# A decoder layer on one core: out projection with the model's columns on partitions, the second norm's square put onto the MLP's sums later, x1 turned by VectorE blocks and HBM

## The chip, the cores and the metric

The kernel runs on one core of one Trainium2 chip. The metric is the device time of one execution in microseconds (us); the time before is the median of three runs. Engines are named as in the profile: PE is TensorE, DVE is VectorE, ACT is ScalarE, POOL is GpSimd, and SP is the queue that issues nearly all DMAs.

## The reference

One layer of a causal decoder, for 1024 tokens (T) of 1024 columns (D), in float32. With `DEPTH = 1` only layer 0 runs: gated linear attention (GLA), then an MLP, then a last norm.

```python
x = x + gla_mixer(rms_norm(x, norm_mix), ...)      # ends in (o * silu(r)) @ w_out
x = x + sqrelu_mlp(rms_norm(x, norm_ffn), w1, w2)  # square(relu(h @ w1)) @ w2
return rms_norm(x, final_norm)
```

`rms_norm(x, g)` is x times rstd = (mean of x squared + 1e-6) to the power -1/2, one number per token, times g, one number per column. The x after the mixer is called x1 below. Two things follow from the formula and are used by the change: a positive factor per token passes through relu, and comes out of the square as its square. So the MLP of rstd * (x1 * g) is rstd squared times the MLP of x1 * g.

## The kernel before

The last part of the kernel, from line 908, is one out projection (1024 x 1024 x 1024) and an MLP whose 4096 hidden columns are worked in four chunks (NC = 4) of 1024; each chunk is an up projection (1024 x 1024 x 1024) and a down projection of the same size, whose sums are added up over the chunks. These nine matrix products are the entries 0 to 8 of the list `plan`: the out projection is 0, the up projections are 1, 3, 5, 7, the down projections 2, 4, 6, 8.

Each product is cut in halves along all three sizes (blocks "11", "12", "21", "22") and made by Strassen-Winograd's scheme: seven block products instead of eight. A block product is a **step** of 48 matmuls of 128x128 by 128x512: four lanes (128 rows of the result), four slices of the inner size, and three matmuls for each of these, because every float32 operand is split into a high and a low float32r part (`split`, lines 79 to 82: ScalarE copies the high part, VectorE subtracts for the low part). A step is named by its product number n; `PLAIN` (line 140) runs them in the order 0, 5, 1, 2, 3, 4, 6, `USUAL` in the order of their numbers. "Step 5" in the texts below is the position in this order, counted from 0. Before a step its two operands are made: the block sums of the scheme (`Side.sums`, line 180, each a 128x1024 instruction on VectorE or GpSimd) and the split into tiles called `big`. There are eight `big` tiles, four to a step, so the operands of a step can be made while the step before it runs, when the step before that has let go of its tiles.

A product's left side is either the weights or the activations, given by the flag s_form and the order in the tuple of `plan`: it sets which formulas of `form` (line 147) each side uses. After a step, its **sink** takes each lane's result out of PSUM: onto x1 (`onto_x1`, line 936), into the hidden tiles (`hidden_into`, line 980) or into the last norm (`final`, line 1028).

The order on TensorE is written by hand: it is the order of the program text, and `hooks` puts further work at a place (product, step, lane, slice) or behind a step's preparation ("then"). On the other engines and on SP the compiler's scheduler orders the instructions by readiness and by place in the text; they run in that order.

Around the change the work is this:

- The out projection has the tokens on partitions: the gated output og (four `hq` tiles, called qk there) is the left side, w_out the right side. Its sums are added onto x1, which is x loaded into eight `vx` tiles, one for each 128 tokens (`load_x1`, line 932).
- When a token tile is complete, `normed` (line 960) makes its square sum on ScalarE (L963), rstd (`rstd_of`, lines 103 to 114), and x1 times rstd on VectorE (L965). Then `transposed` (line 968) turns it by TensorE: 64 transposes of 128x128 (L975), whose results ScalarE scales with g_ffn into four `hq` tiles xraw (L977). The `hooks` of lines 1077 to 1079 place these transposes in the last steps of the out projection and the first steps of the first up projection.
- The first up projection makes its right-hand operands from xraw. `keep_w` (line 1005) stores all 14 split tiles (1 MB each) in HBM as xw, and the later three up projections only load them again, two for each step (`Stored`, lines 1009 to 1021, L1019).
- Every down projection adds its sums onto x1 by `onto_x1` (L940), the last one inside `final`, which squares, norms and stores the rows.

Buffers that matter: `hq` 4, `vx` 8, `raw` 2, `g4` 6, `big` 8 (line 56). In PSUM there are eight banks, `gl` 5 and `mm` 3.

Of the kernel before, what the change touches and what calls it, by code (L numbers as in the profile page):

```python
# [16 lines left out]
P = 128  # L17
T = 1024
# [30 lines left out]
def hybrid_trunk(ctx: ExitStack, tc: tile.TileContext, x, xT, w_head, w_r, w_gk, w_up,  # L49
# [69 lines left out]
    def run(general):  # L119
# [8 lines left out]
        def half(hf):  # L128
            return slice(hf * 512, hf * 512 + 512)
# [778 lines left out]
        def from_out(a, b, kh, dst):  # L908

            load = nc.sync.dma_start(dst.rearrange("p (h n) -> p h n", h=2),  # L910
                              w_out[4 * b + 2 * a:4 * b + 2 * a + 2, :, half(kh)].rearrange("h p n -> p h n"))
            order_after(tc, load, box["xt", 7, R_LAST[0]], wait=False)

        def from_up(c):
# [12 lines left out]
            return bring  # L927


        x1 = {}  # L930

        def load_x1(t):
            x1[t] = new("vx")
            order_after(tc, nc.sync.dma_start(x1[t], x[t * P:(t + 1) * P, :]), box["xt", 7, R_LAST[1]], wait=False)

        def onto_x1(n, lane, p_):
            e, dh = int(PART[n][0]) - 1, int(PART[n][1]) - 1
            xd = x1[4 * e + lane][:, half(dh)]
            with tc.high_priority():
                return dve.tensor_tensor(xd, p_, xd, op=ALU.add)  # L940

        def og_block(a, b):
            return lambda kp, n: qk[kp // 2, b - 1].rearrange("p (h t) -> p h t", h=2)[:, :, half(a - 1)]

        so = Side(True, {f"{a}{b}": og_block(a, b) for a in (1, 2) for b in (1, 2)}, dve, pair_temp, late=True)
        wo = weight_side(False, from_out, dve, "vx")
        wo.load("11")
        wo.load("21")
        ops = [[so.split(0), wo.split(0)]]
        for t in range(4):  # L950
            load_x1(t)
        wo.load("12")
        wo.load("22")
        for t in range(4, 8):
            load_x1(t)


        xn, xraw = {}, {}

        def normed(t):  # L960
            xt = new("g4")
            with tc.high_priority():
                act.activation(xt, x1[t], AF.Square, accum_out=ss2[:, t:t + 1])  # L963
                rstd_of(rstd2[:, t:t + 1], ss2[:, t:t + 1], 1, D)
                dve.tensor_scalar(xt, x1[t], rstd2[:, t:t + 1], None, op0=ALU.mult)  # L965
            xn[t] = xt

        def transposed(hf, kts):
            for kt in kts:
                b = f"{kt // 4 + 1}{hf + 1}"  # L970
                if b not in xraw:
                    xraw[b] = in_tile(new("hq"))
                p_ = new("mm")
                for c in range(4):
                    pe.transpose(p_[:, c * P:(c + 1) * P], xn[4 * hf + c][:, kt * P:(kt + 1) * P], ident)  # L975
                with tc.high_priority():
                    act.activation(xraw[b](kt % 4, 1)[:, 0, :], p_, AF.Copy, scale=g_ffn[:, kt:kt + 1])  # L977


        def hidden_into(hd):  # L980
# [28 lines left out]
        class Stored:  # L1009
# [5 lines left out]
            def split(self, n):  # L1015
                out = []
                for kh in range(2):
                    w = new("big", F32R)
                    nc.sync.dma_start(w.bitcast(F32), xw[n][kh])  # L1019
                    out.append(kl(w))  # L1020
                return out


        gfin = []
# [3 lines left out]
        def final(n, lane, p_):  # L1028

            e, dh = int(PART[n][0]) - 1, int(PART[n][1]) - 1  # L1030
            t = 4 * e + lane
            xt, rs = x1[t], rstd3[:, t:t + 1]
            onto_x1(n, lane, p_)
            if n in (3, 4):
                y, sq = row[t] = new(ROW[t])[:, 0:D], new("st")
                cs = half(dh)
# [28 lines left out]
        def norm_after(last, e):  # L1065
            def then(n, lane, p_):
                onto_x1(n, lane, p_)
                if n == last:
                    normed(4 * e + lane)
            return then  # L1070

        def load_gfin():
            gfin.append(new("g4"))
            nc.sync.dma_start(gfin[0], g_fin)


        hooks = {(0, 5, 3, 1): (0, (0, 1)), (0, 5, 3, 3): (0, (2, 3)), (0, 6, 0, 3): (0, (4, 5)), (0, 6, 1, 3): (0, (6, 7)),
                 (1, 0, 2, 3): (1, (0, 1)), (1, 0, 3, 1): (1, (2, 3)), (1, 0, 3, 3): (1, (4, 5)), (1, 1, 0, 1): (1, (6, 7))}
        hooks = {k: (g(transposed, *w),) for k, w in hooks.items()}
        hooks[0, 0, 3, 3] = (g(outputs_T, TT - 1, ("mm", "mm")),)  # L1080
        hooks[2 * NC - 2, 0] = (load_gfin,)
        chunks_of(plan, ops, hooks, {(0, 4): norm_after(3, 0), (0, 6): norm_after(6, 1)}, last_by_lane=True)

    flag = sb.tile([P, 1], I32, name="flag")
    with tc.manual_schedule(engines={mybir.EngineType.PE}):
# [67 lines left out]
```

## Time and profile before

| what | value |
|---|---|
| median of three runs | 1005.69 us (1005.55 to 1005.74) |
| the profiled execution | 1004.96 us, its span 1003.7 us |
| TensorE busy | 991.0 us, 99% |
| VectorE, ScalarE, GpSimd busy | 737.1, 554.6, 226.0 us |
| DMA | 176.87 MB in 98956 packets, mean 176 GB/s |
| share of the chain of waits on TensorE | 81%; 1% of it the transposes of L975 |

The profile shows one execution. The span is the time between its first and its last recorded instruction; the execution's own time is a little longer. "Busy" counts the time in which an engine has an instruction running. The chain of waits follows the work that ended last back to what released it each time: only what stands in the chain sets the end. A row of groups gives the source line, the engine, the operation, output and inputs, the shape, the count, the busy time, the mean of one in ns, and the idle time before it with what ended it. "PEclk" is the clock granted to TensorE, in tenths of full speed; it is at full speed nearly throughout.

### The profile page before, as it was taken

How to read it: one execution, taken by the hardware profiler on the slowest of the kernel's cores; microseconds unless marked ns; L12 is line 12 of the kernel's file. 1: busy time of each engine (PE TensorE's matmuls, PEld its weight loads, DVE VectorE, ACT ScalarE, POOL GpSimd, SP SyncE). 2: the span in 40 equal slices, each digit the busy share in tenths (PEclk: the TensorE clock that was granted, in tenths of full speed). 3: DMA queues.
4: the chain of work that ended last, by engine and by line, in shares of the span. 5: the costliest groups of instructions: out<-in, count | busy, mean ns of one | idle time of the engine just before them, and what ended most of it. 6: DMA issues, size and time to landing. Idle time of an engine off the chain costs nothing.

```text
span 1003.7 us, 12278 instructions
## 1 busy us (share of the span) xinstructions
PE 991.0 (99%) x4572; PEld 827.3 (82%) x4572; DVE 737.1 (73%) x899; ACT 554.6 (55%) x842; POOL 226.0 (23%) x142
## 2 busy tenths in 40 slices
PE   9999999999999999999999999999999999999995
PEld 8888878889988888888888888888888888888884
DVE  6995786778899998889873349874349964339965
ACT  7775554787793577666432546332447342456455
POOL 0000110113430000042233141234141224241270
PEclk9999999999999999999999999999999999999998
DMA  9899785576382224761215851214951224960004
GB/s 279 312 333 361 285 295 194 202 245 209 122 302 62 79 92 187 293 251 43 85 46 189 353 209 43 78 49 180 349 225 43 61 65 168 338 236 14 1 1 171
DMA packets 98956, 176.87 MB, mean 176 GB/s; under 512 B 5576, under 2 KB 67144, under 8 KB 87368
## 3 DMA queue, kind: packets, MB, share of 16 engines
q1 hardware_dynamic: 98328, 175.59, 49.0%
q8 instruction: 38, 0.62, 0.3%
q10 hardware_dynamic: 560, 0.40, 0.1%
q14 instruction: 30, 0.25, 0.1%
HBM read 138.23 MB, written 37.75 MB: 175 GB/s over the span
## 4 chain that ended last, share of the span: by engine, by line
PE 81%; ACT 2%; DVE 2%; issue 1%; ACTq 0%; DVEq 0%
PE gl L70 54%; PE mm L70 26%; PE mm L975 1%; PE mm L636 0%; ACT g L696 0%; DVE vx L940 0%; PE mm L715 0%; DVE big L82 0%; ACT wb L81 0%; DVE big L783 0%; ACT g L1045 0%; PE gl L715 0%; DVE g L705 0%; DVE g L675 0%; ACT hq L717 0%
## 5 line engine op out<-in xcount | busy, mean ns | idle before, releaser
L70 PE MATMUL gl<-big,big 128*128 128x512 f32 x2712 | 631.4, 390 | 0.3 <-DVE big L82 0.3
L70 PEld LDWEIGHTS gl<-big,big 128*128 128x128 f32 x2712 | 508.1, 188 | 105.8 <-DVE big L82 0.9
L70 PE MATMUL mm<-big,big 128*128 128x512 f32 x1224 | 288.2, 389 | 0.0
L70 PEld LDWEIGHTS mm<-big,big 128*128 128x128 f32 x1224 | 229.7, 188 | 47.7
L82 DVE TENSOR_TENSOR big<-wa,big 128x1024 fp32r<-128x1024 f32 (+1 forms) x120 | 162.1, 1376 | 103.8 <-ACT big L81 103.7
L81 ACT ACTIVATE big<-wa 128x1024 fp32r<-128x1024 f32 (+1 forms) x120 | 120.6, 1039 | 133.1 <-PE gl L70 63.4
L184 POOL TENSOR_TENSOR wa<-wa,wa 128x1024 f32<-128x1024 f32 x28 | 75.2, 2691 | 160.5 <-DVE big L82 159.6
L184 POOL TENSOR_TENSOR wa<-wa,wb 128x1024 f32<-128x1024 f32 x14 | 42.9, 3065 | 279.2 <-DVE big L82 279.2
L82 DVE TENSOR_TENSOR big<-wb,big 128x1024 fp32r<-128x1024 f32 x48 | 63.4, 1338 | 50.1 <-ACT big L81 50.1
L82 DVE TENSOR_TENSOR big<-hq,big 128x1024 fp32r<-128x1024 f32 x48 | 61.3, 1283 | 42.8 <-ACT big L81 42.8
L81 ACT ACTIVATE big<-wb 128x1024 fp32r<-128x1024 f32 x48 | 49.1, 1053 | 61.7 <-PE mm L70 31.0
L81 ACT ACTIVATE big<-hq 128x1024 fp32r<-128x1024 f32 x48 | 48.7, 1054 | 58.2 <-PE gl L70 32.5
L81 ACT ACTIVATE big<-raw 128x1024 fp32r<-128x1024 f32 x42 | 43.7, 1058 | 52.4 <-DVE raw L184 25.4
L82 DVE TENSOR_TENSOR big<-raw,big 128x1024 fp32r<-128x1024 f32 x42 | 66.8, 1607 | 2.3 <-ACT big L81 2.2
L940 DVE TENSOR_TENSOR vx<-gl,vx 128x512 f32<-128x512 f32 x95 | 63.2, 682 | 4.5 <-PE gl L70 4.3
L184 POOL TENSOR_TENSOR wa<-wb,wa 128x1024 f32<-128x1024 f32 x14 | 41.1, 2946 | 44.7 <-DVE big L82 44.7
L556 POOL COPY top<-g 128x4 f32<-128x4 f32 x8 | 10.1, 1264 | 180.6 <-DVE g L548 180.6
L998 ACT ACTIVATE hq<-hq 128x1024 f32<-128x1024 f32 x24 | 25.4, 1058 | 29.6 <-DVE hq L991 29.6
L678 POOL TENSOR_SCALAR g<-g,est 128x256 f32<-128x256 f32 x28 | 29.1, 1057 | 52.0 <-DVE g L675 33.0
L70 PE MATMUL gl<-wb,wa 128*128 128x256 f32 x180 | 32.1, 310 | 0.0
L940 DVE TENSOR_TENSOR vx<-mm,vx 128x512 f32<-128x512 f32 x45 | 30.1, 681 | 2.0 <-PE mm L70 1.9
L989 ACT ACTIVATE hq<-gl 128x512 f32<-128x512 f32 x36 | 21.3, 592 | 14.6 <-PE gl L70 14.6
(191 smaller groups left out, 834.6 us busy)
## 6 DMA issues: line engine op xcount, KB each, us to landing
big<-xw SPq DMA_DIRECT2D x42, 1024.0 KB, 6.8
big<-xv SPq DMA_DIRECT2D x20, 1024.0 KB, 6.1
xv<-big SPq DMA_DIRECT2D x14, 1024.0 KB, 7.5
xw<-big SPq DMA_DIRECT2D x14, 1024.0 KB, 5.8
wb<-in_w_ff SPq DMA_DIRECT2D x32, 256.0 KB, 3.3
wa<-in_w_ff SPq DMA_DIRECT2D x32, 256.0 KB, 3.4
wa<-in_w_ff SPq DMA_DIRECT2D x16, 512.0 KB, 4.5
wb<-in_w_ff SPq DMA_DIRECT2D x16, 512.0 KB, 4.3
```

Source lines behind the costliest of these rows:

```text
L70: pe.matmul(o, w, m, start=start, stop=stop, skip_group_check=partial)
L81: last["split"] = act.activation(hi, src, AF.Copy)
L82: last["low"] = dve.tensor_tensor(lo, src, f32(hi), op=ALU.subtract)
L184: op = self.eng.tensor_tensor(*(self.ap(b, kp, 2) for b in (o, x_, y_)), op=op)
L556: pool.tensor_copy(top[:, 8 * h + 4 * hf:8 * h + 4 * hf + 4].unsqueeze(2), a[:, :, P - 1:P])
L678: pool.tensor_scalar(S[:, vs], Z[:, vs], g, None, op0=ALU.mult)
L940: return dve.tensor_tensor(xd, p_, xd, op=ALU.add)
L975: pe.transpose(p_[:, c * P:(c + 1) * P], xn[4 * hf + c][:, kt * P:(kt + 1) * P], ident)
L989: act.activation(d, p_, AF.Copy)
L998: act.activation(d2, d2, AF.Relu)
```

## The change

The out projection changes its sides: w_out is now the left side (model columns on partitions) and og the right side, so that its result is x1 turned, x1T. It is added onto x turned, which the host lays out anyway (`load_x1T`, from xT). The 64 transposes, `normed` and `transposed` go away. `times_g` multiplies each finished half tile of x1T by g_ffn (per partition now) straight into xraw. No rstd is applied there: the MLP works on x1 * g.

The MLP's sums go into eight new tiles y (`onto_y`), opened in the first chunk by the sinks' first touch and not lying on x1 any more. x1 is wanted again with tokens on partitions. For this each finished x1T tile is stored to HBM (xh). In the second up projection it is loaded again (`turn_load`), each 32x32 block of it is transposed by VectorE (`turn_blocks`), and four DMAs for each tile (`turn_store`) put the blocks in their places of xm, rows of 32 floats at a time. In the fourth up projection `x1_load` brings xm back by token tiles, and `x1_onto` makes the square sum and rstd, squares rstd, and sets y to y * rstd^2 + x1. The last down projection's sums are multiplied by rstd^2 as they are added (in `final`).

The diff without the removed functions (`load_x1`, `onto_x1`, `normed`, `transposed`, `norm_after` and the old hooks):

```diff
-                              w_out[4 * b + 2 * a:4 * b + 2 * a + 2, :, half(kh)].rearrange("h p n -> p h n"))
+                              w_out[4 * a + 2 * b:4 * a + 2 * b + 2, :, half(kh)].rearrange("h p n -> p h n"))
...
+        def load_x1T(kt):
+            x1T[kt] = new("vx" if kt < 6 else "g4")
+            order_after(tc, nc.sync.dma_start(x1T[kt], xT[kt * P:(kt + 1) * P, :]), box["xt", 7, R_LAST[1]], wait=False)
+        def times_g(name, lane):
+            if name not in xraw:
+                xraw[name] = in_tile(new("hq"))
+            e, hf = int(name[0]) - 1, int(name[1]) - 1
+            kt = 4 * e + lane
+            act.activation(xraw[name](lane, 1)[:, 0, :], x1T[kt][:, half(hf)], AF.Copy, scale=g_ffn[:, kt:kt + 1])
+        def onto_x1T(n, lane, p_):
+            kt, hf = 4 * (int(PART[n][0]) - 1) + lane, int(PART[n][1]) - 1
+            xd = x1T[kt][:, half(hf)]
             with tc.high_priority():
-                return dve.tensor_tensor(xd, p_, xd, op=ALU.add)
+                dve.tensor_tensor(xd, p_, xd, op=ALU.add)
+                if n in (3, 4, 6):
+                    times_g(PART[n], lane)
+            if n in (3, 6):
+                nc.sync.dma_start(xh[kt], x1T[kt])
...
-        so = Side(True, {f"{a}{b}": og_block(a, b) for a in (1, 2) for b in (1, 2)}, dve, pair_temp, late=True)
-        wo = weight_side(False, from_out, dve, "vx")
+        so = Side(False, {f"{a}{b}": og_block(a, b) for a in (1, 2) for b in (1, 2)}, dve, pair_temp, late=True)
+        wo = weight_side(True, from_out, dve, "vx")
...
+        def turn_load(kt):
+            turn[kt] = new("g4")
+            order_after(tc, nc.sync.dma_start(turn[kt], xh[kt]), last["xw"], wait=False)
+        def turn_blocks(kt):
+            u = new("g4")
+            dve.transpose(u, turn[kt])
+            turn[kt] = u
+        def turn_store(kt):
+            u = turn.pop(kt)
+            for q_ in range(4):
+                dst = xm[:, kt * P + 32 * q_:kt * P + 32 * q_ + 32].rearrange("(b i) j -> i b j", i=32)
+                store = nc.sync.dma_start(dst, u[32 * q_:32 * q_ + 32, :].rearrange("p (b j) -> p b j", j=32))
+                order_after(tc, store, last["xw"], wait=False)
...
-                    nc.sync.dma_start(w.bitcast(F32), xw[n][kh])
+                    last["xw"] = nc.sync.dma_start(w.bitcast(F32), xw[n][kh])
...
+        def onto_y(c):
+            def add(n, lane, p_):
+                t, dh = 4 * (int(PART[n][0]) - 1) + lane, int(PART[n][1]) - 1
+                if t not in y_:
+                    y_[t] = new("vx")
+                yd = y_[t][:, half(dh)]
+                with tc.high_priority():
+                    if c == 0 and n in (0, 1, 2, 6):
+                        act.activation(yd, p_, AF.Copy)
+                    else:
+                        dve.tensor_tensor(yd, p_, yd, op=ALU.add)
+            return add
+        def x1_load(t):
+            x1m[t] = new("g4")
+            order_after(tc, nc.sync.dma_start(x1m[t], xm[t * P:(t + 1) * P, :]), last["xw"], wait=False)
+        def x1_onto(t):
+            sq, one_ = new("raw"), slice(t, t + 1)
+            act.activation(sq, x1m[t], AF.Square, accum_out=ss2[:, one_])
+            rstd_of(rstd2[:, one_], ss2[:, one_], 1, D)
+            dve.tensor_tensor(ss2[:, one_], rstd2[:, one_], rstd2[:, one_], op=ALU.mult)
+            dve.scalar_tensor_tensor(y_[t], y_[t], ss2[:, one_], x1m.pop(t), op0=ALU.mult, op1=ALU.add)
...
-            xt, rs = x1[t], rstd3[:, t:t + 1]
-            onto_x1(n, lane, p_)
+            xt, rs = y_[t], rstd3[:, t:t + 1]
+            xd = xt[:, half(dh)]
+            with tc.high_priority():
+                dve.scalar_tensor_tensor(xd, p_, ss2[:, t:t + 1], xd, op0=ALU.mult, op1=ALU.add)
...
-        plan = [(so, wo, 1, onto_x1, PLAIN)]
+        plan = [(wo, so, 0, onto_x1T, PLAIN)]
...
-                         onto_x1 if c < NC - 1 else final, USUAL))
+                         onto_y(c) if c < NC - 1 else final, USUAL))
...
+        for k in range(KT):
+            for i, at, f in ((2 * NC - 6, 6 + k, turn_load), (2 * NC - 6, 7 + k, turn_blocks), (2 * NC - 6, 8 + k, turn_store),
+                             (2 * NC - 2, 5 + k, x1_load), (2 * NC - 2, 7 + k, x1_onto)):
+                hooks.setdefault((i + at // 7, at % 7, "then"), []).append(g(f, k))
```

The last lines give the places: `turn_load` of tile k comes behind the preparation in step 6 of product 2 for k = 0 and one step later for each further tile, `turn_blocks` one step after that and `turn_store` two; `x1_load` begins in step 5 of product 6 and `x1_onto` two steps later. `order_after(..., wait=False)` only sets the order on SP's queue: behind the last xw load that the program has issued by then.

More of the change, by code (lines that the diff above doesn't have):

```diff
@@ L927, in from_down @@
             return bring
[L930 to L938, printed above, removed]
-            with tc.high_priority():
-                return dve.tensor_tensor(xd, p_, xd, op=ALU.add)
+        x1T, xraw = {}, {}
+        xh = [dram.tile([P, T], F32, name=f"xh{k}{int(general)}") for k in range(KT)]
@@ new lines, in run @@
+        xm = dram.tile([T, D], F32, name=f"xm{int(general)}")
+        def load_x1T(kt):
[7 more added lines that the diff above has]
+            act.activation(xraw[name](lane, 1)[:, 0, :], x1T[kt][:, half(hf)], AF.Copy, scale=g_ffn[:, kt:kt + 1])
@@ L942, in og_block @@
+        def onto_x1T(n, lane, p_):
+            kt, hf = 4 * (int(PART[n][0]) - 1) + lane, int(PART[n][1]) - 1
+            xd = x1T[kt][:, half(hf)]
+            with tc.high_priority():
+                dve.tensor_tensor(xd, p_, xd, op=ALU.add)
[3 more added lines that the diff above has]
+                nc.sync.dma_start(xh[kt], x1T[kt])
         def og_block(a, b):
-            return lambda kp, n: qk[kp // 2, b - 1].rearrange("p (h t) -> p h t", h=2)[:, :, half(a - 1)]
@@ L945, in run @@
-        so = Side(True, {f"{a}{b}": og_block(a, b) for a in (1, 2) for b in (1, 2)}, dve, pair_temp, late=True)
-        wo = weight_side(False, from_out, dve, "vx")
+            return lambda kp, n: qk[kp // 2, a - 1].rearrange("p (h t) -> p h t", h=2)[:, :, half(b - 1)]
+        so = Side(False, {f"{a}{b}": og_block(a, b) for a in (1, 2) for b in (1, 2)}, dve, pair_temp, late=True)
+        wo = weight_side(True, from_out, dve, "vx")
         wo.load("11")
+        wo.load("12")
+        ops = [[wo.split(0), so.split(0)]]
@@ L948, in run @@
+        for kt in range(4):
+            load_x1T(kt)
         wo.load("21")
[L949 to L952, printed above, removed]
         wo.load("22")
[L954 to L977, printed above, removed]
+        for kt in range(4, 8):
+            load_x1T(kt)
@@ new lines, in run @@
+        turn = {}
+        def turn_load(kt):
[11 more added lines that the diff above has]
+                order_after(tc, store, last["xw"], wait=False)
@@ L1018, in split @@
                     w = new("big", F32R)
-                    nc.sync.dma_start(w.bitcast(F32), xw[n][kh])
+                    last["xw"] = nc.sync.dma_start(w.bitcast(F32), xw[n][kh])
                     out.append(kl(w))
                 return out
+        y_, x1m = {}, {}
+        def onto_y(c):
[19 more added lines that the diff above has]
+            dve.scalar_tensor_tensor(y_[t], y_[t], ss2[:, one_], x1m.pop(t), op0=ALU.mult, op1=ALU.add)
         gfin = []
@@ L1062, in run @@
             plan.append((Side(True, hd[c], dve, pair_temp), weight_side(False, from_down(c), pool), 1,
-                         onto_x1 if c < NC - 1 else final, USUAL))
[L1065 to L1070, printed above, removed]
+                         onto_y(c) if c < NC - 1 else final, USUAL))
         def load_gfin():
@@ L1074, in load_gfin @@
             nc.sync.dma_start(gfin[0], g_fin)
[L1077 to L1082, printed above, removed]
+        hooks = {(0, 0, 3, 3): [g(outputs_T, TT - 1, ("mm", "mm"))],
+                 (0, 4, "then"): [g(times_g, "11", lane) for lane in range(4)], (2 * NC - 2, 0): [load_gfin]}
+        for k in range(KT):
+            for i, at, f in ((2 * NC - 6, 6 + k, turn_load), (2 * NC - 6, 7 + k, turn_blocks), (2 * NC - 6, 8 + k, turn_store),
+                             (2 * NC - 2, 5 + k, x1_load), (2 * NC - 2, 7 + k, x1_onto)):
+                hooks.setdefault((i + at // 7, at % 7, "then"), []).append(g(f, k))
+        chunks_of(plan, ops, hooks, {}, last_by_lane=True)
     flag = sb.tile([P, 1], I32, name="flag")
```

## The prediction

> **What bounds the kernel now.** I read the page's head first, then what TensorE waited for, then the chain of waits.
>
> ```profile
> span 1003.7 us, 12278 instructions
> ## 1 busy us (share of the span) xinstructions
> PE 991.0 (99%) x4572; PEld 827.3 (82%) x4572; DVE 737.1 (73%) x899; ACT 554.6 (55%) x842; POOL 226.0 (23%) x142
> ```
>
> ```profile
> PE gl L70 <- DVE ones L90: 1.1, 1, 1.1
> PE mm L70 <- DVE vx L483: 0.8, 1, 0.8
> PE gl L70 <- DVE big L82: 0.3, 1, 0.3
> ```
>
> TensorE is busy for 99% of the span, and these three rows are all it ever waited for, 2.2 us. So an instruction taken from TensorE saves its length, and an operand or transfer that comes late costs its lateness, if the other engines have no slack to give. The chain of waits shows what there is to save.
>
> ```profile
> 364.82 0.87 PE mm L975 x8
> ...
> 395.57 0.87 PE mm L975 x8
> ...
> 590.94 34.00 PE gl L70 x150
> ```
>
> The transposes of the second norm (L975) stand in the chain as eight pieces of eight, the first and the last quoted, each 0.87 us. The third row gives the step: 34.00 us for 150 matmuls is 227 ns each, and a step of 48 matmuls takes 10.88 us. It holds three steps and the 6 matmuls after them, and begins step 5 of the second up projection (steps counted from 0). Hence that projection begins at 590.94 - 5 x 10.88 = 536.5.
>
> **The change, part by part.** *TensorE.* The 64 transposes go: 8 x 0.87 = 7.0 us, all in the chain. The out projection keeps its seven products of 48 matmuls; only the roles of weights and activations are exchanged. Sum so far: -7.0 us.
>
> *The norm.* Squares, rstd and one VectorE pass over each token tile leave the stretch between out and up projection; the scaling by g_ffn stays as 16 ScalarE instructions, now from SBUF. What was hidden beside TensorE there becomes less.
>
> *Order of the sums in the out projection.* VectorE is full here:
>
> ```profile
> 322.00:333.00 11.00, 11.00 (x50) 9.09 (x50) 10.95 (x13) 4.02 (x4) 0.00 (x0) 1.00 0.01 1
> 333.00:344.00 11.00, 11.00 (x50) 9.12 (x49) 10.94 (x12) 4.02 (x4) 0.00 (x0) 1.00 0.36 105
> ```
>
> (Columns: stretch, its length, busy us of PE, PE's weight loads, DVE, ACT and POOL, then clock, DMA share and GB/s.) The rows that carry the new VectorE work:
>
> ```profile
> L940 DVE TENSOR_TENSOR vx<-gl,vx 128x512 f32<-128x512 f32 x95 | 63.2, 682 | 4.5 <-PE gl L70 4.3
> ...
> L989 ACT ACTIVATE hq<-gl 128x512 f32<-128x512 f32 x36 | 21.3, 592 | 14.6 <-PE gl L70 14.6
> ...
> L184 DVE TENSOR_TENSOR hq<-hq,hq 128x1024 f32<-128x1024 f32 x10 | 12.2, 1221 | 0.1
> ...
> L965 DVE TENSOR_SCALAR g<-vx,rstd 128x1024 f32<-128x1024 f32 x8 | 5.9, 750 | 0.1
> ...
> L483 DVE SCALAR_TENSOR_TENSOR vx<-gl,tok,vx 128x512 f32<-128x512 f32 x6 | 4.5, 747 | 7.2 <-PE gl L70 7.1
> ...
> L110 DVE SCALAR_TENSOR_TENSOR st<-rstd,st 128x1 f32<-128x1 f32 x8 | 1.7, 214 | 0.0
> ```
>
> By the two forms, both sides together need 16 sums of 1.22 us before and after. Two of them (2.4 us) move from the preparation of step 4 to that of step 2, where it is the weights that get them. Since the 1.22 us a sum are the same and TensorE's last recorded wait there is 0.3 us, I put 0 here, with ends of 0 and 2.4 us.
>
> *First MLP chunk.* Its sums open the new accumulators: 16 of the evictions become ScalarE copies of 0.59 us (L989) in place of VectorE adds of 0.68 us (L940). ScalarE is idle for 7 of 11 us in such steps (4.02 in the windows). Nothing on the path.
>
> *The turn of x1.* Eight stores xh (0.5 MB each) go out at the end of the out projection and nobody waits for them for 150 us. In the second up projection come, for each tile, one load, one VectorE block transpose and four stores, one tile per step. The transpose is not in the trace: its ends are 0.75 us (L965, one source) and twice a sum, 2.4 us; I take 1.22. Either way it lies in the room that VectorE has in these steps:
>
> ```profile
> 550.00:561.00 11.00, 11.00 (x50) 9.13 (x49) 5.99 (x6) 5.06 (x5) 4.60 (x3) 1.00 0.83 316
> 561.00:572.00 11.00, 11.00 (x51) 9.09 (x50) 2.36 (x2) 5.49 (x8) 0.33 (x1) 1.00 0.96 379
> 572.00:583.00 11.00, 11.00 (x50) 9.13 (x49) 2.36 (x2) 4.29 (x6) 5.87 (x3) 1.00 0.48 197
> 583.00:594.00 11.00, 11.00 (x51) 9.09 (x50) 5.67 (x6) 5.77 (x6) 4.61 (x2) 1.00 0.61 224
> 594.00:605.00 11.00, 11.00 (x50) 9.13 (x49) 7.30 (x9) 7.49 (x9) 0.00 (x0) 1.00 0.49 203
> ```
>
> The DMA engines are another matter: these five rows hold (0.83 + 0.96 + 0.48 + 0.61 + 0.49) x 11 = 37.1 us of DMA work in 55 us, and it is what TensorE reads next: each step fetches its two split tiles of xw.
>
> ```profile
> 550.62 0.89 SPq L1019 DMA_DIRECT2D big<-xw  x2
> ...
> 591.60 0.89 SPq L1019 DMA_DIRECT2D big<-xw  x2
> ```
>
> A pair is issued when the step two before its own has freed the buffers, so it has one step to land. On SP's queue the stores stand right behind a pair (the order after last["xw"]); what waits behind a store is the next pair. SP itself also waits for the block transpose before each store, and that has a step's head start. Between the issues at 550.62 (step 2's pair) and 591.60 (step 6's, the last) the change puts four tile loads and the stores of four tiles; the other four tiles' stores follow the last pair and meet only weights for later stages.
>
> The stores write runs of 32 floats, 128 B. Four tiles make 4 x 4 x 1024 packets, 1024 on each of 16 engines. No packet of this kind is in the trace, so I take its price from two isolated stretches:
>
> ```profile
> 488.05 9.41 SPq L918 DMA_DIRECT2D wa<-in_w_ff  x8
> ```
>
> ```profile
> 488.00:503.00 15.00, 15.00 (x68) 12.43 (x67) 11.56 (x13) 5.71 (x6) 0.00 (x0) 1.00 0.49 141
> ```
>
> ```profile
> 579.00:589.00 10.00, 10.00 (x46) 8.29 (x45) 2.37 (x2) 2.94 (x4) 8.53 (x4) 1.00 0.51 210
> ```
>
> The first stretch is eight loads of 256 KB in 512 B runs: 0.49 x 15 = 7.35 us for 256 packets an engine, 28.7 ns each. The second is one xw pair, 2 MB in 8 KB rows: 5.1 us for 16 packets, 319 ns each. By bytes alone a 128 B packet would take a quarter of 28.7, 7.2 ns; as a packet like any other 28.7 ns. A straight line through both sizes (0.0378 ns per byte and 9.4 ns per packet) gives 14.2 ns. I take the line, because it is drawn through both measured sizes, and keep both ends. A tile load (0.5 MB) is a quarter of a pair, 1.28 us.
>
> The last pair decides: all that stands ahead of it in the queue must be through. From 550: 37.1 us of old work, 4 x 1.28 = 5.1 us of loads, 1024 x 14.2 ns = 14.5 us of stores; the first tile of the pair is there 2.55 us before the second: 550 + 37.1 + 5.1 + 14.5 - 2.55 = 604.2. Step 6 begins at 590.94 + 10.88 = 601.8. TensorE stalls 2.3 us (0 at 7.2 ns, 17.2 at 28.7 ns). Sum: -4.7 us.
>
> The Trainium skill, "DMA: Bandwidth & Descriptors", section "Why small descriptors are slow (HBM only)", gives a packet a fixed cost of about 3 cycles beside one for every 32 B. Worked out by that page, 7 cycles against 19 for 512 B, a 128 B packet would be about 10 ns, and the stall would be nil; no packet of this size is in the trace to test it.
>
> *x1 put onto the sums.* In the fourth up projection eight loads of 1.28 us, one per step, meet the same 37.1 us of DMA work: with 8 x 1.28 = 10 us it stays under 55. Each tile then costs VectorE two times 0.747 (L483's form over 1024) and four small ones of 0.214 at most, 2.4 us. The last three fall in steps 5 and 6 and in step 0 of the last down projection, where one stage earlier VectorE looks like this:
>
> ```profile
> 616.00:626.00 10.00, 10.00 (x46) 8.29 (x45) 9.82 (x7) 4.02 (x4) 4.42 (x2) 1.00 0.00 0
> 626.00:637.00 11.00, 11.00 (x50) 9.11 (x49) 11.00 (x8) 4.14 (x4) 6.66 (x2) 1.00 0.01 1
> ```
>
> ```profile
> 634.46 12.24 PE gl L70 x54
> ```
>
> ```profile
> 639.74 2.35 DVE L82 TENSOR_TENSOR big<-wa,big 128x1024 fp32r<-128x1024 f32 x2
> ```
>
> It is full, but ahead: the operands of the step that begins at 634.46 + 10.88 = 645.3 are done at 642.1, 3.2 us early. Three tiles are 7.2 us. Ends: 0, and 7.2 - 3.2 = 4.0. I take 0, since the steps before have 4 to 8 us free (the rows up to 605) and an instruction that is ready there is not held to its place.
>
> *End.* The last eviction is 0.747 in place of 0.682: +0.07 us.
>
> Total: -7.0 + 2.3 + 0.07 = -4.6 us. The profiled execution took 1004.96 us (span 1003.7 and 1.3 around it), the median of the runs is 1005.69, 0.73 above. So 1000.4 for a run like the profiled one, and **1001.1** beside the median.
>
> **The rivals.** *Stores wholly hidden.* Below 11.9 ns a packet the last pair is in time; then 1005.69 - 6.9 = 998.8. For it: the line's slope is nearly the pure rate. Chance 0.12.
>
> *The stores become the bound (slower).* If a 128 B packet costs as much as one of 512 B, 28.7 ns, each tile's stores take 7.3 us, and with a pair and a tile load a step has 13.7 us of DMA work for 10.88 us. TensorE then waits for xw, 17.2 us in all: 1005.69 - 6.9 + 17.2 = 1016. It turns to a loss at 18.6 ns a packet. For it: 561 to 572 already runs at 0.96. Against: the fixed part fitted is only a third of 28.7. Chance 0.24, spread from 1006 to 1016.
>
> *Two passes a packet.* If a short write to HBM is read and written back, the price is twice 28.7: 58.8 us of stores, a stall of 46.6 us, 1045. No row speaks for it. The Trainium skill, "DMA: Bandwidth & Descriptors", section "Specifications", says that below 512 B the DMA engine does a read-modify-write; by that rule this would be the case to expect. No run here shows it. Chance 0.04.
>
> *VectorE takes TensorE's place in the last chunk.* The three tiles pile up on full steps: 4.0 us, 1005. For it: 11.00 of 11. Against: 3.2 us of lead. Chance 0.10.
>
> *The change doesn't give what it removes.* In the out projection VectorE is at 10.95 of 11; the moved sums may make TensorE wait 2.4 us: 1003.5. Chance 0.08.
>
> **How the numbers follow.** The forecast itself has 0.42. Below it lies 998.8, so the range begins at 998.5; above, it must take in about half of the second rival, to 1013, so that no more than 0.2 is left out. A difference of 0.2%, 2 us, is about what a measurement here can tell. Faster by more: 0.42 + 0.12, and a little of the last rival, 0.55; within: 0.17; slower: 0.28. The likeliest case's own range is 998.5 to 1003.5.
>
> **What would show it.** No L975 in the chain, and PE busy about 7 us less. The new packets under 512 B (32768 of them) and the DMA share from 547 to 600 near 1. If the stores are cheap, TensorE's waits stay near 2 us; if they are dear, a wait of TensorE for DMA on big<-xw in the steps 3 to 6 of the second up projection, and the time from xw's issue to landing above 10 us. TensorE waiting for VectorE in the last down projection or in the out projection would mean the later rivals. I am wrong in the main step if no row of TensorE waiting for xw exists and the time still does not fall by 4 us.

## The result, and the profile after

The changed kernel takes 1010.27 us (median of 7 runs, 1008.34 to 1012.21) where the kernel before takes 1005.55 (7 runs beside it): a ratio of 1.0046, 95% interval 1.0034 to 1.0058. It is 4.7 us slower, with an interval of 3.4 to 5.8. The profiled execution took 1010.57 us, its span is 1008.7.

The head of the page after:

```profile
span 1008.7 us, 12239 instructions
PE 986.9 (98%) x4508; PEld 821.5 (81%) x4508; DVE 752.5 (75%) x899; ACT 564.9 (56%) x858; POOL 229.3 (23%) x142
DMA packets 135694, 193.65 MB, mean 192 GB/s; under 512 B 39240, under 2 KB 100808, under 8 KB 124104
```

TensorE has its 64 instructions less, and yet the span is 5.0 us longer, so TensorE must wait, or run slower, somewhere. What it waited for (line, what ended the wait, us in total, times, longest):

```profile
PE gl L70 <- DMA big<-xw: 4.5, 1, 4.5
PE mm L715 <- DVE g L705: 1.5, 1, 1.5
PE gl L70 <- DVE big L82: 1.3, 2, 1.0
PE gl L70 <- DVE ones L90: 1.1, 1, 1.1
PE mm L70 <- DVE vx L483: 0.8, 1, 0.8
PE gl L70 <- ACT big L81: 0.6, 1, 0.6
```

The first two rows are new, and they are the largest. Of the others the last is new too, and the third was 0.3 us before; experiment 12 comes back to them. The first row is the wait that the prediction's main step speaks of. It stands in the chain of waits like this:

```profile
522.03 23.12 PE gl L70 x102
...
587.31 5.14 PE gl L70 x23
592.45 10.14 DMA big<-xw
602.59 0.14 issue
602.73 26.07 PE gl L70 x102
```

Step 5 of the second up projection begins at 587.14, so step 6 was due at 587.14 + 10.88 = 598.02. The last xw pair was issued at 592.45 and landed 10.14 us later; step 6 began at 602.73, 4.7 us late. The last row holds a second loss: its 102 matmuls took 26.07 us, while the same 102 took 23.12 in the first row. That is 2.95 us more, with no wait in it. The windows tell why (after the counts: the granted clock, the DMA share, GB/s):

```profile
597.00:602.00 5.00, 1.19 (x6) 0.65 (x4) 4.30 (x4) 4.37 (x6) 5.00 (x3) 0.96 1.04 417
602.00:607.00 5.00, 4.27 (x10) 3.44 (x11) 5.00 (x2) 2.88 (x4) 5.00 (x2) 0.50 0.99 249
607.00:612.00 5.00, 5.00 (x20) 4.01 (x20) 4.97 (x5) 0.85 (x1) 0.00 (x1) 0.85 0.99 292
612.00:617.00 5.00, 5.00 (x24) 4.14 (x23) 5.00 (x5) 4.91 (x9) 0.00 (x0) 1.00 1.07 206
```

The clock is at half right after the wait: 10 matmuls in 4.27 us, where 24 fit into 5 us at full speed. By the means of the four rows it was at half from 601.6 to 608.5. TensorE worked for 5.7 us of that, and at half speed that is 2.9 us lost.

The second new wait stands at the out projection's beginning. ScalarE's timeline, first of before, then of after, at the end of the attention:

```profile
293.89 1.09 ACT L81 ACTIVATE big<-hq 128x1024 fp32r<-128x1024 f32 x1
...
297.05 0.37 ACT L696 ACTIVATE g<-gl 128x256 f32<-128x256 f32 x1
...
301.41 1.10 ACT L81 ACTIVATE big<-wb 128x1024 fp32r<-128x1024 f32 x1
```

```profile
298.18 1.06 ACT L81 ACTIVATE big<-wb 128x1024 fp32r<-128x1024 f32 x1 [2.92 <-DMA wb<-in_w_out]
...
300.46 0.37 ACT L696 ACTIVATE g<-gl 128x256 f32<-128x256 f32 x1
```

```profile
301.04 1.41 PE L715 MATMUL mm<-ident,g 128*128 128x128 f32 x4 [1.51 <-DVE g L705]
```

Before, ScalarE split the activations (hq, long there) and came to the weights (wb) at the end. After, the weights' split stands first in its order, and its DMA has not landed: ScalarE stands still for 2.92 us, and behind it in order are the squares of L696, which the last chunk's norm (VectorE, L705) and the last transposes (TensorE, L715) need.

The time by places, from landmarks in the two profiled executions: the stretch from the first transposes of L636 to the last of L715 takes 76.79 us before and 78.53 after (+1.74); from there to the last step's beginning 683.14 and 684.02 (+0.88, which is -6.6 for the transposes, +4.54 for the wait, +2.95 for the clock). That is +2.6. The other 2.4 of the profiled executions' 5.0 lie ahead of L636 (222.53 and 223.76) and behind the last step's beginning (21.2 and 22.4).

### The profile page after: what moved, and what is told of

Its sections match the earlier page's. It is cut to its first block, busy times and chain, and to the rows that moved or that the text cites. A ratio compares the mean times of both kernels' runs of the same rounds, so it can differ in the third digit from the quotient of the medians.

```text
span 1008.7 us, 12239 instructions
## 1 busy us (share of the span) xinstructions
PE 986.9 (98%) x4508; PEld 821.5 (81%) x4508; DVE 752.5 (75%) x899; ACT 564.9 (56%) x858; POOL 229.3 (23%) x142
## 4 chain that ended last, share of the span: by engine, by line
PE 78%; DVE 2%; DMA 2%; ACT 1%; issue 1%; SPq 0%; DVEq 0%; ACTq 0%
PE gl L70 53%; PE mm L70 24%; DMA big<-xw 1%; DMA wb<-in_w_out 1%; DVE big L82 1%; DVE vx L1074 0%; PE mm L636 0%; DMA wb<-in_w_ff 0%; ACT g L696 0%; PE mm L715 0%; ACT wb L81 0%; DVE vx L950 0%; PE gl L715 0%; DVE g L1094 0%; DVE g L705 0%
## 5 line engine op out<-in xcount | busy, mean ns | idle before, releaser
L82 DVE TENSOR_TENSOR big<-wa,big 128x1024 fp32r<-128x1024 f32 (+1 forms) x118 | 156.7, 1353 | 85.1 <-ACT big L81 81.3
L81 ACT ACTIVATE big<-wa 128x1024 fp32r<-128x1024 f32 (+1 forms) x118 | 118.3, 1039 | 116.1 <-PE gl L70 59.3
L184 POOL TENSOR_TENSOR wa<-wa,wa 128x1024 f32<-128x1024 f32 x28 | 78.8, 2821 | 145.7 <-DVE big L82 144.9
L82 DVE TENSOR_TENSOR big<-wb,big 128x1024 fp32r<-128x1024 f32 x50 | 63.3, 1284 | 34.8 <-ACT big L81 34.8
L82 DVE TENSOR_TENSOR big<-hq,big 128x1024 fp32r<-128x1024 f32 x48 | 61.4, 1291 | 34.9 <-ACT big L81 34.8
L81 ACT ACTIVATE big<-wb 128x1024 fp32r<-128x1024 f32 x50 | 51.0, 1052 | 58.2 <-PE gl L70 26.6
L81 ACT ACTIVATE big<-hq 128x1024 fp32r<-128x1024 f32 x48 | 48.6, 1052 | 45.4 <-PE gl L70 21.9
L81 ACT ACTIVATE big<-raw 128x1024 fp32r<-128x1024 f32 x42 | 43.3, 1056 | 52.2 <-DVE raw L184 22.1
L82 DVE TENSOR_TENSOR big<-raw,big 128x1024 fp32r<-128x1024 f32 x42 | 67.2, 1620 | 4.5 <-ACT big L81 4.3
L1000 ACT ACTIVATE hq<-gl 128x512 f32<-128x512 f32 x36 | 21.3, 593 | 20.2 <-PE gl L70 20.1
L1047 DVE TENSOR_TENSOR vx<-gl,vx 128x512 f32<-128x512 f32 x44 | 29.1, 681 | 0.9 <-PE gl L70 0.8
L70 PEld LDWEIGHTS gl<-wb,wa 128*128 128x128 f32 x180 | 26.3, 190 | 2.0
```

Source lines behind the costliest of these rows:

```text
L70: pe.matmul(o, w, m, start=start, stop=stop, skip_group_check=partial)
L81: last["split"] = act.activation(hi, src, AF.Copy)
L82: last["low"] = dve.tensor_tensor(lo, src, f32(hi), op=ALU.subtract)
L184: op = self.eng.tensor_tensor(*(self.ap(b, kp, 2) for b in (o, x_, y_)), op=op)
L1000: act.activation(d, p_, AF.Copy)
L1047: dve.tensor_tensor(yd, p_, yd, op=ALU.add)
```

## The experiments

All but the last are edits of the changed kernel. Times are medians; the kernel before ran on the same chip.

**1. The turn nine steps earlier.** In the program the loads, transposes and stores of the turn begin behind step 4 of the first up projection, in place of step 6 of the first down projection; only the last of them meet the xw pairs of the second up projection. That is nine steps; where the expectation of experiment 5 says seven, it is the same edit. (Not shown below: what comes before the first xw load has no load to be ordered behind, and is left unordered.)

```diff
-            for i, at, f in ((2 * NC - 6, 6 + k, turn_load), (2 * NC - 6, 7 + k, turn_blocks), (2 * NC - 6, 8 + k, turn_store),
+            for i, at, f in ((2 * NC - 7, 4 + k, turn_load), (2 * NC - 7, 5 + k, turn_blocks), (2 * NC - 7, 6 + k, turn_store),
```

> The turn of x1 (tile loads, block transposes, stores) begins some nine steps earlier, so that nearly all of it lies beside the first down projection, where the DMA engines were busy for 27% of the time. Theory 1 (the stores crowd the DMA queue ahead of the last xw pair of the second up projection): the wait of 4.5 us for xw goes, and with it the stretch at a granted clock of 0.69 (102 matmuls in 26.07 us where 23.12 is usual, 2.95 us): 1010.3 - 4.7 - 2.95 = 1002.6 us. Rival (the extra time sits in the rest of the change, the wait only takes the place of another one): 1007 or more, with a new wait of TensorE elsewhere.

Measured: 1002.93 us (1001.03 to 1005.4), ratio to before 0.9976 (0.9965 to 0.9987), 7.3 us less than the changed kernel. The wait for xw is gone, and the stretch in question runs at its old pace:

```profile
585.71 34.00 PE gl L70 x150
```

This is step 5 and all that follows it, without a gap, 227 ns a matmul. 4.54 of wait and 2.95 of clock are 7.5 us, so both losses belong to this one place.

**2. The same bytes in long rows.** Place and bytes of the stores are kept, but each tile goes out in one DMA of 4 KB rows, and its blocks are not put in their places.

```diff
-            for q_ in range(4):
-                dst = xm[:, kt * P + 32 * q_:kt * P + 32 * q_ + 32].rearrange("(b i) j -> i b j", i=32)
-                store = nc.sync.dma_start(dst, u[32 * q_:32 * q_ + 32, :].rearrange("p (b j) -> p b j", j=32))
-                order_after(tc, store, last["xw"], wait=False)
+            store = nc.sync.dma_start(xm[kt * P:(kt + 1) * P, :], u)
+            order_after(tc, store, last["xw"], wait=False)
```

> Each turned tile is stored as it stands, in one DMA of 128 rows of 4 KB, in place of four DMAs in runs of 128 B: the same bytes and the same place on the queue, but the blocks are not put in their places, so x1 is left scrambled. Theory 1 with the packet size as cause (a tile's stores took 3.5 us of DMA time alone, 512 KB in rows 1.3): four tiles free 8.8 us ahead of the last pair, the wait of 4.7 us goes, 1002.6 us. Rival (bytes or the mere number of transfers are the cause): the wait stays within 1 us, 1009 to 1011.

Measured: 1000.7 us (1000.14 to 1002.66), ratio 0.9955 (0.9937 to 0.9973), and no wait for xw. So it is neither the 4 MB nor the transposes' place that makes the pair late; it is that a tile goes out as 4096 packets in four DMAs, where here it is 128 rows in one. This edit changes packets and issues together. That the packets' time is the cause is argued, from their price (experiment 6, and the section on why the prediction was wrong) and from DMA engines that were busy at 0.97. The time is 1.9 us below the expected one and 2.2 below that of experiment 1, though the profiled executions of the two took 1000.84 and 1001.03 us; what sets the medians apart was not found.

**3. The old order of preparation in the out projection.** "x", "X" are the sums and the split of the activations, "W", "n" the split and the next sums of the weights, here for step 1.

```diff
-        chunks_of(plan, ops, hooks, {}, last_by_lane=True)
+        chunks_of(plan, ops, hooks, {}, last_by_lane=True, turns={(0, 1): ("x", "X", "W", "n")})
```

> Only the order in which the two operands of the out projection's second step are prepared is put back as it was before the change: gated output first, then weights. Theory 2 (ScalarE stands in order before the split of the weights' tile that is still on its way, 2.92 us, and the last chunk's squares and the transposes behind it come late): TensorE's wait of 1.5 us at L715 goes, 1.8 us less, 1008.5 us; the wait for xw stays. Rival (VectorE is full there, and the sums moved forward are what is late): the wait moves to the next step and the time stays at 1010.

Measured: 1007.89 us (1006.77 to 1012.32), ratio 1.0028 (1.0017 to 1.004), 2.4 less than the changed kernel. TensorE's waits there:

```profile
PE gl L70 <- DMA big<-xw: 4.2, 1, 4.2
PE gl L70 <- DVE ones L90: 1.1, 1, 1.1
PE mm L70 <- DVE vx L483: 0.8, 1, 0.8
PE gl L70 <- DVE big L82: 0.7, 2, 0.4
```

The row of L715 is gone, the one of xw stays: the two losses are independent. From L636 to L715 it takes 76.79 us, as before. The size of this loss varies: in the other traces with the changed order the wait at L715 is 0.9 us (experiment 1), 1.0 (2 and 6) and 0.3 (4), in place of 1.5.

**4. The xw loads ahead of the stores.** Another way to have the pairs in time: they get high priority on SP's queue.

```diff
-                    last["xw"] = nc.sync.dma_start(w.bitcast(F32), xw[n][kh])
+                    with tc.high_priority():
+                        last["xw"] = nc.sync.dma_start(w.bitcast(F32), xw[n][kh])
```

> Only the place of the xw loads on SP's queue is changed: they get priority, so that the four weight loads that stood directly ahead of the last pair (512 KB each, 1.3 us) come behind it. Theory 1 in its narrow form (what stands ahead of the last pair in the queue decides): 4 x 1.3 = 5.2 us less ahead of it, the wait of 4.7 us goes, 1002.6 us. Rival (the DMA engines have more work than time whatever the order): the wait moves to another pair or to the weights, 1007 or more.

Measured: 1022.61 us (1020.89 to 1027.33), ratio 1.0178 (1.0145 to 1.0211): the expectation failed. The rival's number held (1007 or more), but not its reason, more DMA work than time: the DMA engines had room. SP works in order; with the next pair in front it stood waiting for that pair's buffers (28.8 us between 540 and 610, in the changed kernel 0.5), and the stores and everything behind them waited too.

```profile
566.00:577.00 11.00, 11.00 (x50) 9.13 (x49) 2.36 (x2) 4.29 (x6) 0.00 (x0) 1.00 0.54 194
```

```profile
PE gl L70 <- ACT big L81: 6.8, 2, 6.3
PE gl L70 <- DVE big L82: 6.0, 4, 3.6
PE gl L70 <- DMA big<-xw: 2.3, 1, 2.3
```

The DMA engines were at 0.54 in a stretch where the changed kernel has 0.94 to 1.00, and the down projection's weights (L925), issued at 590.37 in the changed kernel, went out at 607.34. TensorE then waited 15 us by these three rows, 12.8 of them for the splits of tiles that came late and 2.3 for xw.

**5. Both repairs together** (the edits of 1 and 3).

> Both repairs together: the turn of x1 seven steps earlier, and the order of preparation of the out projection's step 0 as it was. Theory: the two losses lie apart (the wait for xw and the clock behind it in the second up projection, and the wait of the transposes of L715 behind ScalarE at the out projection's beginning), so both gains are kept: 1002.9 less 1.8 to 2.4, 1000.5 to 1001.1, no wait of TensorE for big<-xw and none at L715 over 0.2 us. It would be the fastest of the versions that do the whole turn, some 4.5 us ahead of the kernel before. Rival: the wait at L715 only shifts other work of ScalarE and VectorE, and its gain is lost again in the out projection's first steps: 1002.5 to 1003.

Measured: 1000.55 us (1000.28 to 1001.42), ratio 0.9947 (0.9929 to 0.9964): 5 us faster than the kernel before, the fastest version that does the whole turn. TensorE's waits:

```profile
PE gl L70 <- DVE ones L90: 1.1, 1, 1.1
PE mm L70 <- DVE vx L483: 0.8, 1, 0.8
PE gl L70 <- DVE big L82: 0.7, 2, 0.4
PE mm L70 <- DVE hq L1005: 0.3, 1, 0.3
```

**6. Every store twice.** Each of the turn's stores is issued a second time, to another tensor in HBM.

```diff
+                for to in (xm, xm2):
-                dst = xm[:, kt * P + 32 * q_:kt * P + 32 * q_ + 32].rearrange("(b i) j -> i b j", i=32)
+                    dst = to[:, kt * P + 32 * q_:kt * P + 32 * q_ + 32].rearrange("(b i) j -> i b j", i=32)
```

> Every store of the turned x1 is issued twice, the second time to a tensor that nobody reads; all else as in the changed kernel. Theory (a price per packet of 13.75 ns on each of 16 engines, and a queue of DMA work in front of the last xw pair): 1024 packets more an engine ahead of it, 14.1 us; step 6 of the second up projection begins 14 to 15 us later than in the changed kernel, the wait being spread over two or three steps, and each wait over some 3 us costs 2 to 3 us more by a lowered clock: 1024 to 1031 us. Rival (the wait comes from SP's being held at issues and from the order of the queue, not from the packets' time): the number of issues ahead of the pair doubles but the time behind them is not 14 us; a rise under 8 us or over 25 us would speak for that.

Measured: 1027.42 us, one run. From its timeline of TensorE, and from its chain:

```profile
566.23 12.76 PE L70 MATMUL gl<-big,big 128*128 128x512 f32 x48 [2.02 <-DMA big<-xw]
...
595.70 13.83 PE L70 MATMUL gl<-big,big 128*128 128x512 f32 x48 [4.16 <-DMA big<-xw]
615.86 26.23 PE L70 MATMUL gl<-big,big 128*128 128x512 f32 x102 [6.32 <-DMA big<-xw]
```

```profile
520.70 16.33 PE gl L70 x72
```

From the row at 520.70, which is the place of the changed kernel's row at 522.03, to step 6 it takes 95.16 us, there 80.70: 14.46 us more for 1024 more packets on each engine, 14.1 ns a packet. The price per packet holds also under load. The first of the waits shown, 2.02 us, is short, and yet the 48 matmuls behind it took 12.76 us in place of 10.88: the clock fell here too, to a mean of 0.73 from 565 to 570.

**7 and 8. A wait without small packets.** On the version of experiment 5, plain copies of 0.5 MB between HBM tensors stand ahead of the last xw pair, in the third (product 5) and in the fourth up projection (product 7).

```diff
+        def delay(n):
+            for k in range(n):
+                no = dram.tile([P, T], F32, name=f"no{n}_{k}_{int(general)}")
+                order_after(tc, nc.sync.dma_start(no, xh[k % KT]), last["xw"], wait=False)
+        for i, n in {5: 10, 7: 12}.items():
+            hooks.setdefault((i, 4, "then"), []).append(g(delay, n))
```

The second of the two has 14 and 20 copies.

> The version with both repairs, in which TensorE waits for no xw, gets plain copies of 0.5 MB from HBM to HBM (long rows, no small packets) on SP's queue ahead of the last xw pair: 10 in the third up projection, 12 in the fourth. At 1.28 us a copy (a tile load's price) the waits would be about 0.7 and 4.5 us; if a copy costs twice that, about 13 and 19. Theory: the clock falls because TensorE stood still, whatever it waited for. Behind a wait over some 3 us the next 100 matmuls take 2 to 3 us longer than 227 ns each, behind one under 1.5 us none. Rival: the fall belongs to the stream of 128 B stores, which is not there: the granted clock stays at 1.00 behind every wait.

> As the one before, with 14 copies in the third up projection and 20 in the fourth: waits 5 and 10 us longer than there. Theory: a longer wait costs in addition the same 2 to 4 us of a lowered clock, not in proportion to the wait. Rival: the loss of clock grows with the wait; or, without the 128 B stores, none.

Measured: 1021.13 and 1040.0 us, one run each. TensorE's waits were 6.25 and 10.21 us, and 11.88 and 22.64. The longest one in the windows:

```profile
915.00:920.00 5.00, 1.20 (x6) 0.66 (x4) 4.30 (x5) 4.37 (x6) 0.00 (x0) 0.94 1.04 315
920.00:925.00 5.00, 0.00 (x0) 0.00 (x0) 4.97 (x5) 2.90 (x4) 0.00 (x0) 0.50 0.93 295
...
935.00:940.00 5.00, 1.15 (x3) 0.99 (x4) 0.00 (x0) 0.00 (x0) 0.00 (x0) 0.50 0.94 365
940.00:945.00 5.00, 5.00 (x17) 3.93 (x16) 0.00 (x0) 0.00 (x0) 0.00 (x0) 0.67 0.86 337
945.00:950.00 5.00, 5.00 (x24) 4.14 (x23) 2.22 (x2) 3.28 (x5) 0.00 (x0) 1.00 0.00 0
```

No 128 B packet of the turn is near, and the clock falls all the same: to 0.50 from about 3 us after TensorE stopped, and back to 1.00 some microseconds after it started again.

**9. The turn left out** of the version of experiment 5.

```diff
-            for i, at, f in ((2 * NC - 7, 4 + k, turn_load), (2 * NC - 7, 5 + k, turn_blocks), (2 * NC - 7, 6 + k, turn_store),
+            for i, at, f in (
...
-            order_after(tc, nc.sync.dma_start(x1m[t], xm[t * P:(t + 1) * P, :]), last["xw"], wait=False)
+            order_after(tc, nc.sync.dma_start(x1m[t], xh[t]), last["xw"], wait=False)
```

> The version with both repairs, and the turn left out: no load, block transpose or store of it; the fourth up projection loads xh itself, so that x1 is put onto the sums unturned. Theory: with both repairs the turn is wholly hidden beside TensorE, so leaving it out gains nothing that can be measured: 1000.0 to 1001.0 (the version with the turn: 1000.55). Rival: the turn still costs something where it now lies (its stores' traffic or the eight block transposes on VectorE): 998.8 to 999.5, the forecast's first rival.

Measured: 999.84 us (999.55 to 1000.46), ratio 0.994 (0.9927 to 0.9954), beside 0.9947 (0.9929 to 0.9964) with the turn: no difference that can be measured. The time lies between the two forecasts and decides for neither. Nine steps earlier the turn is hidden, all but 0.6 us that the landmarks show (676.55 us from L715 to the last step, 677.19 with the turn).

**10 and 11. Short waits.** The edit of 7 with 7 and 7 copies, and with 8 and 6.

> As the two kernels with plain copies ahead of the last xw pair, with 7 copies in the third up projection and 7 in the fourth. By the waits there (6.25 us with 10 copies and 11.88 with 14 in the third, 10.21 with 12 and 22.64 with 20 in the fourth: 1.41 and 1.55 us a copy) TensorE waits about 2.0 and 2.5 us. Theory: the clock falls only behind a wait longer than some length between 1.5 us (no fall behind it so far) and 3.6 us (a fall); if that length is under 2 us both waits lose 1.8 to 3 us more, if it is over 2.5 us neither does: total 1000.55 + 4.5 and 0 to 6 more. Rival: the loss grows smoothly with the wait: 1 us behind each.

> As the one before, with 8 copies in the third up projection and 6 in the fourth: waits of about 3.4 and 0.9 us. Theory: a fall of the clock behind the first, costing 1.8 to 3 us, and none behind the second: 1000.55 + 4.3 + 1.8 to 3 = 1006.7 to 1007.9. Rival: a loss in proportion to the wait, about 1.7 and 0.4 us.

Measured: 1002.0 and 1002.97 us, one run each. The waits came out shorter than worked out, the price per copy not being constant: in the first 0.92 us in the fourth up projection and none over 0.8 in the third, in the second 1.66 us in the third and none in the fourth. The clock stayed at 1.00. So neither of the two runs has a wait of the length that they were to test; experiments 4 and 6 have. Behind experiment 6's wait of 2.02 us the clock fell, and behind experiment 4's of 2.29 us for xw:

```profile
725.34 2.90 PE L70 MATMUL gl<-big,big 128*128 128x512 f32 x6 [2.29 <-DMA big<-xw]
```

```profile
725.00:730.00 5.00, 4.66 (x14) 3.75 (x15) 0.00 (x0) 1.95 (x2) 1.04 (x1) 0.66 1.02 408
```

The 6 matmuls took 2.90 us in place of 1.36, and a granted clock with a mean of 0.66 over 5 us is 3.4 us at half clock. So in these runs the length from which the clock falls lies between 1.66 us and 2.02.

**12. The kernel before, once more.**

> The kernel before, profiled once more. In the profiled executions of the changed kernel and of the experiments the code ahead of the out projection, which is the same text in all, reaches the first transposes of L636 at 222.1 to 224.2 us, and the time from the last step's beginning to the span's end is 20.8 to 22.4; in the one profile of before they are 222.5 and 21.2. Theory: both vary from execution to execution of whatever kernel, and this profile lies elsewhere in the same ranges; then the some 2 us of difference between the sums by landmarks and the medians are not a cost of the change that has a place in the code. Rival: it gives 222.5 and 21.2 again, within 0.2 us; then the change has a small cost at the beginning or the end as well.

Measured: 1004.88 us; 222.42 us to L636, 21.3 from the last step's beginning to the end. The rival held as far as two profiles can say: both repeat within 0.2 us. In the twelve profiles of the changed kernel and its variants the first number is 222.09 to 224.17, mean 223.35, and the second 20.8 to 22.4, mean 21.4. So versions of the changed kernel seem to lose about 0.9 us on average ahead of L636. In the changed kernel's profile it is lost in the first 35 us, where TensorE waits 0.6 us for ACT big L81 and 1.0 us for DVE big L82 at the first operands (rows three and six of its waits). The program text is the same there, and what delays those operands was not found.

## Why the prediction was wrong

The forecast was 1001.1 us, faster; the result is 1010.27, slower, though still inside the range. Three terms failed: the stall of 2.3 us was 2.2 us too small, the clock behind it (2.95 us) had no term, and the order of the sums, put at 0, cost 1.74 us. The steps in their order:

*TensorE, -7.0: right.* From the out projection's first step to one place in the first down projection (the row at 522.03) it takes 219.38 us in place of 225.98, -6.6, with 0.33 us of wait for VectorE in one step of it.

*Order of the sums in the out projection, "I put 0 here, with ends of 0 and 2.4 us": failed.* It cost 1.74 us in the trace, and undoing the order alone gained 2.4 in the medians. The size lies inside the ends, but the mechanism is another. I counted sums on VectorE; the exchange of sides also changes which operand is split first, and the weights' split put ScalarE behind a DMA that had not landed, with the attention's last norm queued behind it. A step that is moved in an engine's order has to be asked what it waits for there, not only how long it takes.

*The stores' price, 14.2 ns by the line: right.* One tile's stores alone in a stretch of the changed kernel:

```profile
623.00:634.00 11.00, 11.00 (x50) 9.13 (x49) 10.87 (x10) 4.11 (x5) 6.38 (x3) 1.00 0.32 49
```

0.32 x 11 = 3.5 us for 256 packets an engine, 13.75 ns each; experiment 6 gives 14.1 under load. The line was drawn through loads of 512 B and 8 KB, and no row said that it would hold for stores of 128 B, so there is some luck in this. The rival by packet count alone (28.7 ns) and the one of two passes (57 ns) both fall: experiment 2 shows that the cutting into runs of 128 B is the cause, but the price is this one. Of the Trainium skill's two rules that the prediction set beside it, the fixed cost in "DMA: Bandwidth & Descriptors", section "Why small descriptors are slow (HBM only)" was the nearer one (an estimate of about 10 ns by it). The other, in section "Specifications", a read-modify-write below 512 B, does not show as a second pass in these prices.

*"TensorE stalls 2.3 us": mis-sized, 4.5 to 4.7 measured.* From the start of the count (550 there, 546.2 on the clock of after) to the landing:

```profile
546.20:602.60 56.40, 51.98 (x230) 42.73 (x228) 25.91 (x25) 26.72 (x30) 12.05 (x6) 0.99 0.97 305
```

0.97 x 56.4 = 54.7 us of DMA work, where I had 37.1 + 5.1 + 14.5 - 2.55 = 54.15. The work was right within 1%. The other 1.7 us is DMA time not used: I reckoned with engines that are never idle, a share of 1.00 for 55 us. (The share is not a sharp measure: rows above reach 1.04 and 1.07.) SP's own timeline shows what may be one reason why they are not kept full:

```profile
580.37 8.26 SPq L987 DMA_DIRECT2D xm<-g  x4
588.67 1.59 SPq L976 DMA_DIRECT2D g<-xh  x1
590.37 0.91 SPq L925 DMA_DIRECT2D wb<-in_w_ff  x2
591.37 0.99 SPq L925 DMA_DIRECT2D wa<-in_w_ff  x2
592.45 1.10 SPq L1030 DMA_DIRECT2D big<-xw  x2
```

The pair could have been issued when step 5 began, at 587.14 (591.60 against 590.94 before); it was issued at 592.45, 5.3 us later. SP was still issuing the fourth tile's stores until 588.6, and a tile load and four weight loads stood between. How much of the 1.7 us that makes was not measured by itself.

*After the stall: the step that was missing, 2.95 us.* The sum took a stall at its length. Beside the waits over 0.8 us in the MLP, what the 102 matmuls behind each took (23.12 us without a wait); left out are five that stand close to another wait, experiment 4's 6.30 and 1.71 us and experiment 6's 2.02, 1.40 and 4.16:

| wait, us | what came ahead | 102 matmuls, us | more, us |
|---|---|---|---|
| 0.92 | 7 copies | 23.40 | 0.3 |
| 1.66 | 8 copies | 23.37 | 0.3 |
| 2.29 | xw, late in experiment 4 | 24.86 | 1.7 |
| 3.10 | a split, experiment 6 | 25.18 | 2.1 |
| 3.57 | a split, experiment 4 | 25.01 | 1.9 |
| 4.22 | stores (experiment 3) | 24.99 | 1.9 |
| 4.54 | stores (changed kernel) | 26.07 | 3.0 |
| 6.25 | 10 copies | 25.34 | 2.2 |
| 6.32 | doubled stores | 26.23 | 3.1 |
| 10.21 | 12 copies | 24.90 | 1.8 |
| 11.88 | 14 copies | 25.37 | 2.3 |
| 22.64 | 20 copies | 25.48 | 2.4 |

A wait of up to 1.7 us costs 0.3 us beyond its length; one of 2.3 us or more costs 1.7 to 3.1 us beyond it, whatever the length and whatever was waited for. The Trainium skill, "TensorE: Matmul & The Clock Gate", section "What's actually happening", has this rule: the clock goes to half after an idle window of about 3.4 us and back after a busy one, and the windows run freely. The traces agree on the half clock, and a loss that scatters with no relation to the wait fits windows that run freely. On the length they differ, and the measurement decides: the clock fell behind waits of 2.02 and 2.29 us, well under 3.4. So the stall of 2.3 us that I forecast would probably have cost some 1.7 to 1.9 us more as well, by the waits of that length in experiments 4 and 6: the term was missing whatever the stall's size.

*Block transpose, 1.22 us: right* (1.24), though the price was taken from another operation, and hidden:

```profile
L980 DVE STREAM_TRANSPOSE g<-g 128x1024 f32<-128x1024 f32 x8 | 9.9, 1239 | 9.2 <-DMA g<-xh 9.2
L1060 DVE SCALAR_TENSOR_TENSOR vx<-vx,ss,g 128x1024 f32<-128x1024 f32 x8 | 11.8, 1476 | 0.3
```

*x1 put onto the sums, 0: right.* The second row is the pass that I took as two times 0.747; TensorE has no wait in the fourth up projection or the last down projection. The rival of VectorE in the last chunk falls.

*The rivals.* "The stores become the bound" came nearest in its sign and place, a wait for xw in the second up projection, but its reason was a price that the packets do not have, and its turning point of 18.6 ns was never reached. That the result lies inside the range is therefore luck: its upper end was drawn for this rival. The loss is made of three smaller things instead: 2.2 us more stall than forecast, 2.95 of clock, 1.74 of ScalarE's order; with the 0.4 that the transposes gave less, 7.3 us. Of the 9.2 us between forecast and result that leaves 1.9; by the landmarks they lie ahead of L636 and behind the last step's beginning, and their cause stays open.

## What to carry to other kernels

A transfer that is to be hidden beside a busy queue needs room: count the queue at less than full use, and ask whether the added work may start earlier, since here the same work nine steps earlier cost nothing that could be measured. Price a stall of TensorE over about 2 us at its length and 2 to 3 us more. When two operands exchange their roles, follow their order on every in-order engine to the DMA that each waits for, and do not repair such a queue by putting the next load in front: what that load waits for then stops everything behind it.

## What the hardware showed that was not expected

The clock after a wait, in the table above; it fell behind waits from 2.0 us on. And the issue of a DMA itself, which held SP up among the stores (times in ns: least, median, most):

```profile
L987 SPq DMA_DIRECT2D xm<-g x32: 303/570/7525, 548.0 to 646.2; - x32
```

Half of the 32 issues took 0.57 us or less, but one took 7.5 us, time in which everything else in SP's order waited. Small packets are not the only thing that slows SP: in experiment 8 no issue of a long copy took over 0.85 us, but from the first of the 20 copies to the pair behind them SP took 28.9 us.
